# The down product as seven block products in two sets of four banks, its operands streamed

## The chip, the cores and the metric

The kernel runs on one NeuronCore of a Trainium2 chip. The metric is the device time of one execution in microseconds (us), from start to end. Engines are named as in the profile: PE is TensorE (PEld its weight loads), DVE is VectorE, ACT is ScalarE, POOL is GpSimd, SP is SyncE, which issues nearly all transfers.

## What is computed

One layer of an encoder trunk for two request groups g = 0 and 1 (1024 tokens, width 1024), all in float32. The change touches the last third, the feed-forward block:

```python
def conv_glu_ffn(x, w_up, conv_w, conv_b, w_down):
    u = x @ w_up                                  # (1024, 1024) @ (1024, 5632)
    gate, val = jnp.split(u, 2, axis=-1)          # 2816 columns each
    gate = lax.conv_general_dilated(gate, ...) + conv_b     # depthwise, width 3, over tokens
    h = jax.nn.gelu(gate, approximate=False) * val
    return h @ w_down                             # (1024, 2816) @ (2816, 1024)

# in encoder():
x = layer_norm(alpha * x + conv_glu_ffn(x, ...), ln3_g, ln3_b)
```

## The kernel before

Precision: each float32 operand is split into a high part (rounded to the matmul's float32r) and a remainder, and each product is three matmuls: high x high, high x remainder, remainder x high (`mm3`, L128). A split is a copy (ACT or POOL) and a subtraction (DVE or POOL): `split` (L113) and `wsplit` (L120).

The order of the work is the text's, put through a scheduler of the framework, which moves instructions of each engine ahead of others where its own clock says that they are ready first; waits follow from the use of tiles. So the streams of the engines in the trace are not in the order of the text everywhere.

Tiles that matter here: `raw` (L82), three buffers of 4 KB per partition, in which matrices land; `wts` (L1265), six buffers of 8 KB for split weights; fourteen single `slots` of 8 KB (L1270); `resid` (L81), two buffers of 16 KB; PSUM: two each of `pS` (two banks), `pT` and `pO` (one bank), eight banks in all.

The up product (`ffn_up`, L1059) runs over 22 column blocks f of 128 gate and 128 value columns. Each is already computed as seven block products (a scheme with seven instead of eight products of half-size blocks): the blocks of the activation and their sums lie split in the slots; the sums of the weight blocks are made per f in `up_sums` (L1022) from two tiles of `raw` (a11 and a12; a21 and a22), on POOL, and split in `up_weights` (L1041). The products run in the order 6, 1, 7, 5, 2, 4, 3, each 12 matmuls of 128x512; DVE and ACT put the results together (`prod`, L1090). `end` (L1116) makes one block h[f] of 128 features x 1024 tokens in a tile `d` (two buffers) and writes it to DRAM (hD, L1125). During f the weights of f + 1 are made. The working tile of a block (`res`, 16 KB) is one of two that alternate.

The down product (`ffn_down`, L1183) is a plain one. `h_in` (L1163) fetches h[f] (512 KB), splits it with ACT and DVE into a slot; `wd_in` (L1172) fetches two 128-row blocks of one half of w_down's columns, and POOL splits them into `wts`. There are four rounds: (f 0 to 11, columns 0 to 511), (f 0 to 11, columns 512 to 1023), (f 12 to 21, columns 0 to 511), each with f outside and the eight token tiles inside, so that all eight banks are in use; and (f 12 to 21, columns 512 to 1023) with the token tile outside, so that each token tile can be normed and written as it is done (`layernorm`, L798). Each round ends with eight evacuations (`evac`, L1200), DVE operations that add a bank to y; y is loaded from DRAM (yD) at the start, 2 MB twice, and multiplied by the previous norm's gain on DVE.

After the down product of group 0, `phase_in` (L288) of group 1 follows, whose input weights are fetched into `raw` and split into `wts` and whose inputs go to tiles that lie where the slots lay.

## Time and profile before

| what | value |
|---|---|
| median of 3 runs | 3237.38 us (3234.4 to 3240.18) |
| the profiled execution | 3236.86 us, its span 3234.9 us |
| PE busy | 3148.2 us, 97% of the span |
| PEld, DVE, POOL, ACT busy | 83%, 55%, 48%, 38% |
| mean granted clock of PE | 0.989 of full |
| moved by DMA | 351.64 MB, 109 GB/s over the span |
| up product | about 1040 to 1465 us (g = 0), about 2551 to 2988 us (g = 1) |
| down product | about 1465 to 1704 us (g = 0), about 2988 to 3226 us (g = 1) |

The busy line says which engine is in use; the chain of work that ended last says on whose instructions the end depends; the list of waits says for what an engine stood; the timeline shows single instructions with their start and duration. The duration of a matmul there includes its pipeline: its rate is read from the distance of starts.

### The profile page before, as it was taken

What the parts mean: (1) busy time and instruction counts of PE and PEld (TensorE: products, weight loads), DVE (VectorE), ACT (ScalarE), POOL (GpSimd) and SP (SyncE); (2) the same over time, 40 slices, a digit from 0 to 9 for tenths busy, and PEclk for the clock granted to TensorE, in tenths of its full rate; (3) what the DMA queues carried; (4) which work ended last, traced back from release to release, by engine and by line L of the source; (5) the groups of instructions that cost most, each with busy time, mean ns of one, the idle gap of its engine ahead of it and who ended that gap; (6) DMA issues with size and microseconds to landing.
All of it is one profiled execution on the core that took longest, in us unless ns stands there. A gap on an engine that the chain in (4) does not pass through costs nothing.

```text
span 3234.9 us, 43051 instructions
## 1 busy us (share of the span) xinstructions
PE 3148.2 (97%) x16425; PEld 2672.9 (83%) x16425; DVE 1769.0 (55%) x2991; ACT 1217.2 (38%) x2373; POOL 1565.4 (48%) x1165
## 2 busy tenths in 40 slices
PE   8999999999999999999998989999999899999998
PEld 6888889888887888888887889888888788888887
DVE  4152167884536756666235246688444766665614
ACT  2122167882334433331101127687243443333101
POOL 7373512783423655543436451288342465554442
PEclk9999999999999999999999999999999999999999
DMA  8455486003112222236415367501311223224521
GB/s 266 120 150 194 162 219 172 14 8 118 47 52 72 78 81 89 79 111 221 128 55 183 117 169 176 142 17 31 101 49 46 79 78 95 82 79 143 179 95 52
DMA packets 292867, 351.64 MB, mean 109 GB/s; under 512 B 18012, under 2 KB 211764, under 8 KB 291508
## 3 DMA queue, kind: packets, MB, share of 16 engines
q1 hardware_dynamic: 290068, 340.43, 34.7%
q10 hardware_dynamic: 2592, 8.46, 0.7%
q8 instruction: 129, 2.11, 0.3%
q14 instruction: 78, 0.64, 0.1%
HBM read 252.24 MB, written 100.79 MB: 109 GB/s over the span
## 4 chain that ended last, share of the span: by engine, by line
PE 89%; DVE 4%; DMA 3%; POOL 2%; issue 1%; ACT 1%; SPq 0%; ACTq 0%; POOLq 0%; DVEq 0%
PE pS L1095 11%; PE pT L1095 7%; PE pO L1095 7%; PE pO L130 7%; PE pO L132 7%; PE pO L131 7%; PE pT L132 7%; PE pT L130 7%; PE pT L131 7%; PE pO L720 3%; PE pS L693 3%; PE pO L611 3%; PE pT L709 3%; PE pS L132 2%; PE pS L131 2%; PE pS L130 2%
## 5 line engine op out<-in xcount | busy, mean ns | idle before, releaser
L126 POOL TENSOR_TENSOR wts<-raw,wts 128x512 fp32r<-128x512 f32 (+1 forms) x229 | 467.2, 2046 | 239.8 <-ACT wts L109 234.9
L1095 PE MATMUL pS<-t,wts 128*128 128x512 f32 (+1 forms) x1656 | 378.7, 382 | 0.9 <-DVE res L1104 0.9
L1095 PEld LDWEIGHTS pS<-t,wts 128*128 128x128 f32 x1656 | 304.4, 190 | 60.5 <-DVE res L1104 1.6
L130 PE MATMUL pT<-wts,t 128*128 128x512 f32 (+1 forms) x840 | 327.8, 390 | 9.3 <-ACT wts L109 8.9
L130 PE MATMUL pO<-wts,t 128*128 128x512 f32 (+1 forms) x840 | 328.7, 392 | 3.5 <-ACT t L109 2.6
L131 PE MATMUL pO<-wts,t 128*128 128x512 f32 (+1 forms) x840 | 325.5, 388 | 4.2 <-POOL wts L126 4.2
L132 PE MATMUL pO<-wts,t 128*128 128x512 f32 (+1 forms) x840 | 325.6, 388 | 2.9 <-POOL t L126 1.7
L132 PE MATMUL pT<-wts,t 128*128 128x512 f32 (+1 forms) x840 | 325.6, 388 | 0.2 <-POOL t L126 0.2
L131 PE MATMUL pT<-wts,t 128*128 128x512 f32 (+1 forms) x840 | 325.2, 387 | 0.5 <-DVE wts L126 0.5
L1095 PE MATMUL pT<-t,wts 128*128 128x512 f32 (+1 forms) x1104 | 260.3, 385 | 9.8 <-ACT t L109 5.9
L125 POOL TENSOR_SCALAR wts<-raw 128x1024 fp32r<-128x1024 f32 (+1 forms) x88 | 100.6, 1147 | 335.3 <-DMA raw<-w_down 199.7
L1095 PE MATMUL pO<-t,wts 128*128 128x512 f32 (+1 forms) x1104 | 257.2, 382 | 0.4 <-ACT t L109 0.4
L1095 PEld LDWEIGHTS pT<-t,wts 128*128 128x128 f32 x1104 | 204.5, 192 | 50.7 <-ACT t L109 6.3
L1095 PEld LDWEIGHTS pO<-t,wts 128*128 128x128 f32 x1104 | 203.3, 190 | 40.1 <-ACT t L109 0.8
L130 PEld LDWEIGHTS pT<-wts,t 128*128 128x128 f32 x840 | 158.4, 189 | 39.8 <-ACT wts L109 8.9
L132 PEld LDWEIGHTS pO<-wts,t 128*128 128x128 f32 x840 | 158.6, 189 | 35.6 <-POOL t L126 2.2
L130 PEld LDWEIGHTS pO<-wts,t 128*128 128x128 f32 x840 | 158.9, 189 | 35.1 <-ACT t L109 3.9
L131 PEld LDWEIGHTS pO<-wts,t 128*128 128x128 f32 x840 | 158.7, 189 | 35.1 <-POOL wts L126 4.5
L132 PEld LDWEIGHTS pT<-wts,t 128*128 128x128 f32 x840 | 158.3, 188 | 31.8 <-POOL t L126 0.4
L131 PEld LDWEIGHTS pT<-wts,t 128*128 128x128 f32 x840 | 158.4, 189 | 31.4 <-DVE wts L126 1.0
L696 DVE TENSOR_REDUCE mn<-pS 128x1 f32<-128x1024 f32 x128 | 155.9, 1218 | 38.3 <-PE pS L693 36.9
L126 DVE TENSOR_TENSOR wts<-xr,wts 128x512 fp32r<-128x512 f32 x86 | 105.7, 1230 | 107.7 <-ACT wts L109 107.7
(274 smaller groups left out, 6714.7 us busy)
## 6 DMA issues: line engine op xcount, KB each, us to landing
raw<-w_up SPq DMA_DIRECT2D x88, 512.0 KB, 4.1
hD<-d SPq DMA_DIRECT2D x44, 512.0 KB, 5.0
raw<-hD SPq DMA_DIRECT2D x44, 512.0 KB, 3.7
raw<-w_down SPq DMA_DIRECT2D x44, 512.0 KB, 3.7
raw<-w_in SPq DMA_DIRECT2D x32, 512.0 KB, 4.8
kst<-ka SPq DMA_DIRECT2D x32, 512.0 KB, 8.8
qa<-vs SPq DMA_DIRECT2D x16, 512.0 KB, 3.9
ka<-vs SPq DMA_DIRECT2D x16, 512.0 KB, 4.3
```

Of the source, the lines that this page charges most:

```text
L125: nc.gpsimd.tensor_scalar(hi, raw, 1.0, 0.0, op0=ALU.mult, op1=ALU.add)
L126: return (nc.vector if dve else nc.gpsimd).tensor_sub(lo, raw, hi.bitcast(F32))
L130: mm(out, sh, mh, start=start, stop=False)
L131: mm(out, sh, ml, start=False, stop=False)
L132: mm(out, sl, mh, start=False, stop=stop)
L611: nc.tensor.matmul(po[:, n * 64:(n + 1) * 64], pt[:, n, j], v, start=j == 0, stop=j == 1)
L693: nc.tensor.matmul(p[:, ns], q[:, ct * 128:(ct + 1) * 128], ks[:, hl, ns], start=hl == 0, stop=hl == 1)
L696: nc.vector.tensor_reduce(mn, p, axis=X, op=ALU.min)
L709: nc.tensor.transpose(p[:, c * 128:(c + 1) * 128], s[:, k * 128:(k + 1) * 128], self.ident)
L720: nc.tensor.matmul(po[:, :256], bd["v"][:, k, h // 4], hl[l][:, k].rearrange("p a b -> p (a b)"), start=k == 0 and l == 0, stop=k == 7 and ...
L1095: nc.tensor.matmul(p, w[:, x, k], b[l][:, k, cs], start=i in (1, 6, 7, 5) and k + x + l == 0, stop=k == 3 and x == 1, skip_group_check=True)
```

## The change

The down product becomes a product of seven blocks as well. Its operands are halves of the tokens (left, right) by the even and odd 128-row blocks of the 2816 features, and the even and odd row blocks by halves of the columns of w_down. Each of the seven products has 11 steps (one for each pair of row blocks); a step has one 128x512 operand of h (or a sum of such) and one 128x512 operand of w_down (or a sum), and 4 x 3 matmuls.

- `end` collects two blocks d0 and d1; at each odd f it makes three sums of their halves and one difference in place (two on POOL, two on DVE), writes d1 and d0 to hD and the three further blocks to a new DRAM array hS.
- `down_sums`, called at each odd f of group 0 only, fetches two full 128-row blocks of w_down into `raw`, makes four differences in place on POOL, and writes them to a new DRAM array wD, which both groups read.
- `d_in` replaces `h_in` and `wd_in`: for each of the 77 steps it fetches the two operands (two steps at a time into a buffer of `wts`, the first five one at a time into `raw`) and splits both into one slot: one ACT copy of 128x1024, one POOL and one DVE subtraction of 128x512. Up to seven steps are ahead of the matmuls. The slots go round (ten of them for g = 0, fourteen for g = 1).
- The products run in the order 1, 2, 6, 5, 7, 3, 4, alternating between two sets of four banks; products 1, 6, 7, 4 accumulate one upon the other in the first set, 5 and 3 in the second (2 by itself), and after each the four banks are added to y. For g = 1 the last product runs with the token tile outside.
- `layernorm` can take statistics of one half made earlier.

```diff
-            nc.sync.dma_start(hD[f], d)
+            ds.append(d)
+            if f % 2:
+                j, (d0, d1) = f // 2, ds
+                ds.clear()
+                a11, a21, a12, a22 = d0[:, :512], d0[:, 512:], d1[:, :512], d1[:, 512:]
+                s1, s2, s4 = sets[1][:, 3584:], sets[0][:, 3584:], e.u3
+                nc.gpsimd.tensor_add(s1, a21, a22)
+                nc.sync.dma_start(hD[j, 1], d1)
+                nc.gpsimd.tensor_sub(a21, a11, a21)
+                nc.sync.dma_start(hD[j, 0], d0)
+                nc.vector.tensor_sub(s2, s1, a11)
+                nc.vector.tensor_sub(s4, a12, s2)
+                for i, t in enumerate((s1, s2, s4)):
+                    nc.sync.dma_start(hS[j, i], t)
...
+                    if i == 5 and g == 0 and f % 2:
+                        self.down_sums(f // 2, wD)
+                    if f == NFF - 1 and i in (7, 5, 2, 4, 3):
+                        self.d_in(g)
...
+    def down_sums(self, j, wD):
+        nc = self.nc
+        r = []
+        for o in range(2):
+            t = self.raw.tile([128, D], F32, name="raw")
+            nc.sync.dma_start(t, self.a["w_down"][0][(2 * j + o) * 128:(2 * j + o + 1) * 128])
+            r.append(t)
+        b11, b12, b21, b22 = r[0][:, :512], r[0][:, 512:], r[1][:, :512], r[1][:, 512:]
+        nc.gpsimd.tensor_sub(b11, b12, b11)
+        nc.gpsimd.tensor_sub(b12, b22, b12)
+        nc.sync.dma_start(wD[j, 0], r[0])
+        nc.gpsimd.tensor_sub(b22, b22, b11)
+        nc.gpsimd.tensor_sub(b21, b21, b22)
+        nc.sync.dma_start(wD[j, 1], r[1])
+
+    def d_in(self, g):
+        nc = self.nc
+        s = len(self.ds)
+        m, k = divmod(s, self.NK)
+        i = self.SEVEN[m]
+        if not self.dr:
+            n = 1 if s < 5 else min(2, self.NK - k)
+            if s < 5:
+                r = self.raw.tile([128, 1, 2, 512], F32, name="raw")
+            else:
+                r = self.wts.tile([128, 2, 2, 512], F32, name="wts")
+            for x, src in enumerate((self.hsrc[i], self.wsrc[i])):
+                nc.sync.dma_start(r[:, :n, x], src[:, k:k + n])
+            self.dr = [r[:, x] for x in range(n)]
+        r = self.dr.pop(0)
+        ring = (12, 13, 4, 6, 10, 11, 3, 7, 5, 9) + ((8, 0, 1, 2) if g else ())
+        first = (12, 13, 4, 8, 0, 1, 2, 6, 10, 11, 3, 7, 5, 9)
+        t = self.at_slot(first[s] if s < 14 else ring[(s - 14) % len(ring)], [128, 2, 2, 512])
+        self.copy(t[:, 0], r)
+        for x, e in enumerate((nc.gpsimd, nc.vector)):
+            e.tensor_sub(t[:, 1, x], r[:, x], t[:, 0, x].bitcast(F32))
+        self.ds.append(t)
...
+        pa = [self.pA() for _ in range(2)]
+        sets = [[p[:, n * 512:n * 512 + 512] for p in pa for n in range(2)],
+                [self.pT(), self.pO(), self.pT(), self.pO()]]
...
+        def mm(p, m, k, q):
+            i, t = self.SEVEN[m], self.ds[m * self.NK + k]
+            c = slice(q * 128, q * 128 + 128)
+            for x, l in ((0, 0), (0, 1), (1, 0)):
+                nc.tensor.matmul(p, t[:, x, 0, c], t[:, l, 1], start=i in (1, 2, 5) and k + x + l == 0,
+                                 stop=k == self.NK - 1 and x == 1, skip_group_check=True)
...
+        for m, i in enumerate(self.SEVEN):
+            bank = sets[m % 2]
+            if i == 4:
+                gb = self.ln_load(3)
+                if g:
+                    while len(self.ds) < 7 * self.NK:
+                        self.d_in(g)
+                    for q in range(4):
+                        for k in range(self.NK):
+                            mm(bank[q], m, k, q)
+                        finish(q)
+                        evac(i, q, bank[q])
+                        finish(4 + q)
+                    break
+            for k in range(self.NK):
+                s = m * self.NK + k
+                while len(self.ds) < min(s + 7, 7 * self.NK):
+                    self.d_in(g)
+                if m < 2 and 2 <= k < 6:
+                    v = yt(4 * m + k - 2)
                     nc.vector.tensor_mul(v, v, gb[0])
                     nc.vector.tensor_add(v, v, gb[1])
+                if i == 4 and k % 2 and k < 8:
+                    finish(k // 2)
+                for q in range(4):
+                    mm(bank[q], m, k, q)
+            for q in range(4):
+                evac(i, q, bank[q])
+        if not g:
+            for q in range(4):
+                finish(4 + q)
```

`finish` is `layernorm` of one token tile and the write of its output. `SEVEN` is (1, 2, 6, 5, 7, 3, 4), `NK` is 11.

## Rows read from the trace of the kernel before

**Rows 1.** The page: busy time of the engines; the chain that ended last.

```profile
PE 3148.2 (97%) x16425; PEld 2672.9 (83%) x16425; DVE 1769.0 (55%) x2991; ACT 1217.2 (38%) x2373; POOL 1565.4 (48%) x1165
...
PE 89%; DVE 4%; DMA 3%; POOL 2%; issue 1%; ACT 1%; SPq 0%; ACTq 0%; POOLq 0%; DVEq 0%
```

**Rows 2.** Stretches: busy us (instructions) of five engines, clock, DMA share, GB/s.

```profile
1200.00:1300.00 100.00, 100.00 (x443) 82.80 (x442) 61.37 (x64) 39.53 (x60) 56.37 (x37) 1.00 0.25 80
...
1710.00:1720.00 10.00, 8.72 (x30) 6.76 (x30) 9.53 (x7) 3.67 (x4) 10.00 (x6) 0.80 0.80 272
...
3100.00:3200.00 100.00, 100.00 (x443) 82.82 (x442) 30.84 (x46) 7.98 (x7) 44.73 (x26) 1.00 0.21 70
```

**Rows 3.** PE's waits, 1440 to 1725: total us, times, longest; two of four.

```profile
PE pO L131 <- POOL wts L126: 4.2, 1, 4.2
PE pO L132 <- DVE t L115: 1.3, 1, 1.3
...
```

**Rows 4.** Timeline, 1195 to 1240, up product: start, us, instruction, idle before.

```profile
1201.66 9.61 SPq L1028 DMA_DIRECT2D raw<-w_up  x2
...
1200.33 1.30 POOL L126 TENSOR_TENSOR wts<-raw,wts 128x512 fp32r<-128x512 f32 x1 [4.18 <-ACT wts L109]
1205.63 1.29 POOL L1032 TENSOR_TENSOR cs<-raw 128x512 f32<-128x512 f32 x1 [4.00 <-DMA raw<-w_up]
...
1210.83 1.29 POOL L1033 TENSOR_TENSOR xr<-cs,raw 128x512 f32<-128x512 f32 x1
...
1199.77 0.69 DVE L126 TENSOR_TENSOR wts<-cs,wts 128x512 fp32r<-128x512 f32 x1
1201.42 1.29 DVE L1121 SCALAR_TENSOR_TENSOR d<-res,cwt,d 128x1023 f32<-128x1023 f32 x1 [0.97 <-ACT d L1120]
...
1212.82 1.22 DVE L126 TENSOR_TENSOR wts<-xr,wts 128x512 fp32r<-128x512 f32 x1 [2.52 <-ACT wts L109]
...
1212.16 0.63 ACT L109 ACTIVATE wts<-xr 128x512 fp32r<-128x512 f32 x1 [2.00 <-POOL xr L1033]
...
1198.90 5.15 PE L1095 MATMUL pS<-t,wts 128*128 128x512 f32 x22
...
1217.94 5.15 PE L1095 MATMUL pS<-t,wts 128*128 128x512 f32 x22
```

**Rows 5.** Timeline, POOL and DVE, around 1450: two that overlap.

```profile
1448.18 2.41 POOL L126 TENSOR_TENSOR wts<-raw,wts 128x1024 fp32r<-128x1024 f32 x1
...
1448.67 3.00 DVE L1121 SCALAR_TENSOR_TENSOR d<-res,cwt,d 128x1023 f32<-128x1023 f32 x1 [1.36 <-ACT d L1120]
```

**Rows 6.** Timeline: first group's down product begins (PE, SP); PE after its end.

```profile
1456.85 0.39 PE L130 MATMUL pS<-wts,t 128*128 128x512 f32 x1
...
1464.33 2.88 PE L1095 MATMUL pO<-t,wts 128*128 128x512 f32 x12
...
1480.31 0.32 SPq L1125 DMA_DIRECT2D hD<-d  x1
...
1711.11 0.63 PE L132 MATMUL pO<-wts,t 128*128 128x512 f32 x1
1711.54 0.63 PE L130 MATMUL pO<-wts,t 128*128 128x512 f32 x1
```

**Rows 7.** Groups by form, 1480 to 1700: busy us, mean ns, idle before.

```profile
L109 ACT ACTIVATE t<-raw 128x1024 fp32r<-128x1024 f32 x14 | 14.9, 1062 | 109.3 <-PE pO L132 65.6 <-DMA raw<-hD 43.7
```

**Rows 8.** DMA: the page's issues; hD's landing; rates in 1480 to 1620.

```profile
hD<-d SPq DMA_DIRECT2D x44, 512.0 KB, 5.0
...
raw<-w_down SPq DMA_DIRECT2D x44, 512.0 KB, 3.7
...
DMA to landing us min/median/max: 2.6/4.7/10.9
...
GB/s 276 376 401 408 328 13 150 0 234 69 150 167 296 239 50 88 62 139 140 149 181 323 122 150 0 0 0 39 111 149 6 173 222 191 163 54 137 273 150 140
...
res<-yD SPq DMA_DIRECT2D x1, 2048.0 KB, 9.9
```

More of the change, by code (lines that the diff above doesn't have):

```diff
@@ L802, in layernorm @@
         rs = self.small.tile([128, 2], F32, name="brs")
-        st = self.small.tile([128, 2, 6], F32, name="bst")
-        for j in range(2):
+        js = (0,) if st is not None else (0, 1)
+        st = self.small.tile([128, 2, 6], F32, name="bst") if st is None else st
+        for j in js:
             nc.vector.bn_stats(st[:, j], y[:, j * 512:(j + 1) * 512])
@@ L1086, in begin @@
             return e
-        sets, pair = [], []
+        sets, pair, ds = [], [], []
         def prod(e, i, hf=None):
@@ L1183, in ffn_down, with down_src @@
-    def ffn_down(self, B, yD, hD, out):
+    SEVEN = (1, 2, 6, 5, 7, 3, 4)
+    NK = NFF // 2
+    def down_src(self, hD, hS, wD):
+        w = self.a["w_down"][0].rearrange("(j o p) c -> p j o c", p=128, o=2)
+        l, r = slice(0, 512), slice(512, D)
+        hv, sv, tv = [t.rearrange("j i p c -> p j i c") for t in (hD, hS, wD)]
+        self.hsrc = {1: hv[:, :, 0, l], 2: hv[:, :, 1, l], 6: sv[:, :, 1], 5: sv[:, :, 0],
+                     7: hv[:, :, 0, r], 3: sv[:, :, 2], 4: hv[:, :, 1, r]}
+        self.wsrc = {1: w[:, :, 0, l], 2: w[:, :, 1, l], 6: tv[:, :, 1, r], 5: tv[:, :, 0, l],
+                     7: tv[:, :, 0, r], 3: w[:, :, 1, r], 4: tv[:, :, 1, l]}
@@ L1184, in ffn_down @@
+    def ffn_down(self, g, yD, out):
         nc, a = self.nc, self.a
@@ L1205, in evac @@
                 nc.vector.tensor_add(v, v, p)
-        for lo, hi, n in ((0, K0, 0), (0, K0, 1), (K0, NFF, 0)):
-            bank = []
-            for _ in range(2):
-                p = self.pA()
-                bank += [p[:, :512], p[:, 512:], self.pT(), self.pO()]
-            if (lo, n) != (0, 0):
-                self.wd = [None] * (lo // 2)
-            for f in range(lo, hi):
-                if lo == n == 0 and 2 <= f < 2 + NT:
-                    v = yt(f - 2)
+            if i == 7:
+                stats[ct] = self.small.tile([128, 2, 6], F32, name="bs7")
+                nc.vector.bn_stats(stats[ct][:, 1], v)
@@ new lines, in finish @@
+        def finish(ct):
+            self.layernorm(yt(ct), gb, 896 if g and ct >= NT - 2 else 0, stats.get(ct))
+            nc.scalar.dma_start(out[ct * 128:(ct + 1) * 128], yt(ct))
+        for m, i in enumerate(self.SEVEN):
[18 more added lines that the diff above has]
+                    v = yt(4 * m + k - 2)
@@ L1218, in ffn_down @@
                     nc.vector.tensor_mul(v, v, gb[0])
                     nc.vector.tensor_add(v, v, gb[1])
-                if f % 2 == 0 and f // 2 >= len(self.wd):
-                    self.wd_in(n)
-                if n == 0:
-                    while len(hs) <= f:
-                        self.h_in(hD)
-                elif len(hs) < NFF - 1 and len(hs) - 12 <= f - (3 if f > 4 else 0) and not 4 < f < 8:
-                    self.h_in(hD)
-                for ct in range(NT):
-                    mm(bank[ct], f, ct, self.wd, f == lo, f == hi - 1)
@@ L1230, in ffn_down @@
-            for ct in range(NT):
-                evac(bank[ct], ct, n, lo == 0)
-        gb = self.ln_load(3)
-        self.wd = [None] * (K0 // 2)
-        for f in range(K0, NFF, 2):
-            self.wd_in(1, 2 if f == NFF - 2 else None)
-        for ct in range(NT):
-            p = self.pB()
-            for f in range(K0, NFF):
-                mm(p, f, ct, self.wd, f == K0, f == NFF - 1)
-            evac(p, ct, 1, False)
-            self.layernorm(yt(ct), gb, 896 if ct >= NT - 2 else 0)
-            nc.scalar.dma_start(out[ct * 128:(ct + 1) * 128], yt(ct))
+                if i == 4 and k % 2 and k < 8:
+                    finish(k // 2)
@@ L1286, in run @@
                 if "mid" in stages:
[L1287 removed]
+                    yD = dt(f"yD{g}", [NT, 128, D])
+                    hD, hS = dt(f"hD{g}", [NFF // 2, 2, 128, T]), dt(f"hS{g}", [NFF // 2, 3, 128, 512])
                     B, todo = self.phase_mid(g, S, o2s, ob, G, U, yD)
                 if "ffn" in stages:
[L1290 to L1291 removed]
+                    self.ffn_up(g, B, todo, hD, hS, wD)
+                    self.ffn_down(g, yD, a["out0" if g == 0 else "out1"])
             if stages[-1] != "ffn":
```

43 lines of the change are left out of this document (11 added, 32 removed).

## The prediction

> **What bounds the kernel now.** First read is the page's busy line and the shares of the chain that ended last: TensorE is busy 97% of the span and carries 89% of the chain [rows 1]. So the next views are those that say whether TensorE ever waits in the stages that the change touches. In the up product and in the down product it is busy without a break: 100 us of every 100, 443 matmuls each, at full clock [rows 2]. The list of TensorE's waits from the end of the first up product to beyond the first down product has four entries, 6.3 us together, and all lie behind the last down matmul, where the second request group begins [rows 3]; there the clock also falls [rows 2]. So both stages are pure counts of matmuls: what takes matmuls away is worth its full time until some other engine or a queue ends last. The next view is the timeline of one step of the up product. Consecutive steps start at 1198.90 and 1217.94, thus 19.04 us for 84 matmuls (7 products of 12) or **0.2267 us per matmul** [rows 4].
>
> **What is removed.** The down product of one request group now takes 22 x 8 x 2 x 3 = 1056 matmuls, 239.4 us. After, 7 products x 11 steps x 4 x 3 = 924, 209.5 us. The shape is the same (128x128 stationary, 512 columns moving), so I take the same pace. That is 132 x 0.2267 = 29.9 us per group, **-59.9 us** for both.
>
> **The stream in the down product.** After, a step of 12 matmuls lasts 2.72 us and needs 512 KB fetched and one split: an ACT copy of 128x1024 at 1.06 us [rows 7], a GpSimd subtraction of 128x512 at 1.30 us and a VectorE one at 0.69 us (both when alone [rows 4]). Each fits in 2.72 us, with 7 steps of lead. The fetch is 512 KB in 2.72 us, 193 GB/s; in the present down product the queues moved up to 408 GB/s in slices [rows 8]. No cost in steady state. The evacuations fall from 32 to 28 per group and each bank set now has a whole product (30 us) for its four; they cost nothing, and nothing before either, as TensorE never waited on them [rows 3].
>
> **The start of the down product.** Five steps are ready and the next four come through free weight buffers. Step 9, however, needs the left operand of the last pair of columns. Its present counterpart was written out from 1480.31 [rows 6]. After, a GpSimd addition and a subtraction (1.30 each) come ahead: issue 1482.9, landed 5.0 later, the fetch 3.7 [rows 8], ACT 1.06 and GpSimd 1.30: ready at about 1494. The last up product started at 1464.33 [rows 6] and some 2.5 us of down matmuls had already been slipped in by then; so step 9 is due at about 1464.5 + 9 x 2.72 = 1489. 5 us late, unless matmuls of the second product, which need nothing of that pair, stand in front. The kernel's scheduler did reorder across stages like that: a down matmul (its first at 1456.85) stands ahead of the last up product [rows 6]. Bounds 0 to +8 per group (the 5, and a half-clock stretch behind it, priced as below); I take 1.5, **+3 us**. The loads of y (2 MB, 9.9 us each [rows 8]) must now also wait for the sums' writes. They are queued on SP ahead of fetches, and VectorE's multiplications of y by the gain stand ahead of later splits. A rival below.
>
> **The up product: sums of h.** Per pair of column blocks GpSimd gets 2 operations and VectorE 2 more, SP three more writes, 768 KB. Nobody in this stage waits for them but the two d buffers: the block after next can't begin its d before d0 is written, and ACT's copies are queued behind that. Two GpSimd operations and a 5.0 us write end about when the next use comes (19 us after the last); bank reuse leaves a step of slack. Cost with the next item.
>
> **The up product of the first group: sums of the weights.** Four more GpSimd operations per pair, two loads, two writes, and two more tiles from `raw`, which has three. This is the part I trust least. In the trace the ring of three is already what times the weights: the second w_up load of a step goes out (1201.66) the moment GpSimd's split at 1200.33 has released the tile three allocations back; the sum on it starts at 1205.63, the second at 1210.83, ACT's copy at 1212.16, VectorE's remainder ends at 1214.04, and TensorE wants the product at 1217.94 [rows 4]. 3.9 us of slack. After, in every odd step the tile released at 1201.66 goes to a w_down row block instead. On the same clock: load 3.7 -> 1205.4, GpSimd 1.30 -> 1206.7, write, 5.0 as hD's -> 1211.7, only then the w_up load, 4.0 as from 1201.66 to 1205.63 -> 1215.7 (the first two from [rows 8]), two sums 2.6 -> 1218.3, ACT 0.63, VectorE 0.69 to 1.22: 1219.6 to 1220.2. So the first product of the step is **about 2 us late instead of 3.9 early**. Product 1, which needs the other tile, can run first and takes 2.72 us; then nothing is lost. Ten pairs have a step behind them: bounds 0 and +40 (2.2 late and nearly as much again in turns with VectorE); I take 0.8 us a pair, **+8 us**, nearer to the covered end, as the scheduler reorders.
>
> **The turns of VectorE and GpSimd.** While GpSimd's subtraction ran from 1448.18 to 1450.59, VectorE's operation started at 1448.67 and took 3.00 us instead of its 1.29 [rows 4]: it ended 1.1 us behind GpSimd [rows 5]. They take turns. One step of the up product has 7 GpSimd operations at 1.29 (9.0 us) and 4 x 0.69 + 3 x 1.29 (6.6 us) on VectorE with both inputs from tiles in SBUF [rows 4]: 15.6 of 19.04 us, 31.2 of 38.1 per pair. After, the first group adds 6 x 1.30 + 2 x 0.69 = 9.2: **40.4 of 38.1**; the second adds 4.0: 35.2. Up to 1.1 us of each VectorE operation's end evidently lies outside the turn, so the true sum is smaller. Bounds 0 and +25 (2.3 x 11); I take **+2 us**. The Trainium skill, "SBUF — State Buffer", section "Who interferes with whom", has a rule that speaks against the change: a VectorE instruction with two SBUF inputs and a GpSimd instruction that reads SBUF lock each other out fully. The 3.00 us row agrees. By that rule with whole durations the sum would have +25 here, without it 0.
>
> **The end of the first group.** Now the first weights of the next group are split only at the last matmul, since the w_down tiles sit in their buffers until then: 6.3 us of waits [rows 3], and 10 matmuls at about 0.427 instead of 0.2267 (1711.11 to 1711.54), some 2 us [rows 6], at a mean granted clock of 0.80 of 2.4 GHz, thus partly at 1.2 [rows 2]. After, these buffers hold raw data and are done with some 16 us before the end. Against that, four whole layer norms come after the last matmul, GpSimd about 2.4 each, by its 128x1024 operation [rows 5]. Bounds -8 and +6; I take **-4 us**. The end of the second group keeps its chain: evacuation, one statistics half, norm, write.
>
> **Sum.** -59.9 + 3 + 8 + 2 - 4 = -51. The profiled execution took 3236.86 us (span 3234.9 and 2.0 around it), the median of the runs shown is 3237.38, 0.5 above: no correction beyond that. 3237.4 - 51 = **3186 us**.
>
> **Rivals.** *The ring and the turns hidden*: -59.9 + 3 - 4, **3176**. For it: TensorE has no wait at all now [rows 3]. *The ring not covered*: products stay in their order, 4 us for each of ten pairs: -59.9 + 3 + 40 + 2 - 4, **3218**. For it: 3.9 us of slack is all there is [rows 4]. *The turns bind*: +25 in place of 2, **3209**; against it, bank evacuations and ACT's work run beside. *The start starves*: both y loads (19.8 us) ahead of the fetches use up the 7 steps of lead (19 us) and some 10 us per group are lost: -51 + 20, **3206**; against it, before, the stage starts with the same loads and no wait. *Slower than before*: the chain of w_down load, sum, write, w_up load through `raw` sets the step. All other terms give -58.9, so it decides from 5.9 us a pair. With a write at the slowest landing of hD seen, 10.9 instead of 5.0 [rows 8], product 1 not moved: (2.2 + 5.9) x 10 = 81, **3260**. For it, 768 KB and 2 MB more per pair share the queue; against it, DMA moves only about 80 GB/s in this stage [rows 2].
>
> **How the numbers follow.** Forecast 0.40, hidden 0.20, ring uncovered 0.13, turns 0.13, starved start 0.05, slower 0.08; 0.01 for anything else. The range takes the hidden case with the full gain at the group's end and the uncovered ring with a few us more: 3168 to 3228. A measurement of this kernel tells about 0.2% (6.5 us) from no change. Faster 0.87, same 0.04 (the ring between 5 and 6.5 us a pair), slower 0.09.
>
> **What would show it.** Right: 924 matmuls per down product at 0.2267 without a wait; first up product 419 us plus under 20; waits of TensorE on weight splits in odd steps only, and only in the first group. Wrong: waits within the down product on a split or a fetch (the stream does not keep up), waits in the second group's up product (then it is the sums of h or the turns, not the ring), or VectorE and GpSimd both busy without a gap.

## The result, and the profile after

The changed kernel takes 3296.86 us (median of 4 runs, 3293.94 to 3297.42) where the kernel before took 3238.51 beside it: a ratio of 1.018 with the interval 1.0163 to 1.0198. It is **slower by 58 us** where 51 us less was forecast; 3296.86 lies far above the range. The profiled execution took 3297.42 us, its span is 3295.6.

The page of after, engines and chain, to set against [rows 1]:

```profile
PE 3124.1 (95%) x16161; PEld 2640.9 (80%) x16161; DVE 1929.7 (59%) x3135; ACT 1325.8 (40%) x2483; POOL 1831.7 (56%) x1317
...
PE 72%; DMA 8%; POOL 7%; DVE 6%; issue 4%; ACT 2%; SPq 1%; POOLq 0%; ACTq 0%; DVEq 0%
```

The 264 matmuls are gone (16425 to 16161), but PE's busy time fell by 24 us, not by 60: many of those left took longer. Its share of the chain fell from 89% to 72%, and DMA, POOL and DVE took it over. So PE now waits. Where, the list of its waits over the whole span says (total us, times, longest):

```profile
PE pS L1096 <- DVE res L1105: 42.8, 20, 5.0
PE pS L1257 <- ACT t L109: 23.4, 2, 12.8
PE pS L1257 <- POOL t L1233: 17.6, 2, 9.1
...
PE pO L130 <- ACT t L109: 3.1, 1, 3.1
...
PE pO L132 <- DVE t L115: 1.7, 1, 1.7
```

Before, neither stage had such waits ([rows 3] for the time from 1440 on; the few us at the very start of an up product stand in both kernels). L1096 is the up product, L1257 the down product. The last two rows stand at the end of the first group, as in [rows 3]: 4.8 us there, where four before made 6.3. In stretches (columns as in [rows 2]; the first three are the first up product and the start of the first down product, then its steady state, then the second group's up product):

```profile
1200.00:1300.00 100.00, 89.83 (x378) 72.42 (x377) 67.09 (x62) 32.81 (x50) 70.00 (x45) 0.97 0.40 135
1560.00:1580.00 20.00, 4.08 (x7) 1.95 (x7) 20.00 (x21) 10.02 (x10) 13.52 (x1) 0.50 0.99 372
1580.00:1600.00 20.00, 18.72 (x72) 15.31 (x73) 12.54 (x12) 6.37 (x6) 20.00 (x14) 0.84 0.77 278
1640.00:1660.00 20.00, 20.00 (x90) 16.57 (x89) 8.40 (x12) 8.01 (x8) 12.34 (x8) 1.00 0.57 186
2700.00:2800.00 100.00, 100.00 (x443) 82.79 (x442) 70.75 (x71) 38.82 (x60) 65.63 (x43) 1.00 0.32 108
```

Two separate losses are seen. The first group's up product, the only one with sums of weights, does 378 matmuls in 100 us instead of 443; the second group's has no loss. And the down product is at full pace in its steady state (90 matmuls in 20 us), but its start nearly stands still, with the clock at 0.50 (1.2 GHz).

The starts of the matmuls say how much each loss is. From its first matmul to its last, the first group's up product lasts 499.0 us instead of 438.6 (1030.3 to 1529.3, before 1028.2 to 1466.8); the second's lasts 437.1 instead of 436.8. From the last up matmul to the last down matmul, 237.6 us pass instead of 237.3 in the first group, and 236.4 instead of 237.4 in the second. So the starts of the down products eat nearly the whole 60 us of matmuls that were taken away, and the first up product adds 60. Besides, 15.1 us pass from the last matmul to the end of the span, where 9.5 did.

**The up product.** A timeline of 1237 to 1280 in after (start, us, instruction, idle before it), one place of many:

```profile
1237.63 0.34 SPq L1200 DMA_DIRECT2D raw<-w_down  x1
...
1251.95 0.33 SPq L1200 DMA_DIRECT2D raw<-w_down  x1
1255.19 1.38 POOL L1204 TENSOR_TENSOR raw<-raw 128x512 f32<-128x512 f32 x1 [1.05 <-DMA raw<-w_down]
1256.60 0.33 SPq L1205 DMA_DIRECT2D wD<-raw  x1
1259.27 0.38 SPq L1029 DMA_DIRECT2D raw<-w_up  x1
1263.96 1.29 POOL L1033 TENSOR_TENSOR cs<-raw 128x512 f32<-128x512 f32 x1 [4.31 <-DMA raw<-w_up]
1266.52 1.15 ACT L109 ACTIVATE wts<-cs 128x512 fp32r<-128x512 f32 x2 [7.96 <-POOL cs L1035]
1271.14 0.57 ACT L109 ACTIVATE res<-pS 128x512 f32<-128x512 f32 x1
1271.61 2.31 DVE L1122 SCALAR_TENSOR_TENSOR d<-res,cwt,d 128x1023 f32<-128x1023 f32 x1
1273.96 1.28 DVE L1123 SCALAR_TENSOR_TENSOR d<-res,cwt,d 128x1023 f32<-128x1023 f32 x1
1275.16 0.68 DVE L1105 TENSOR_TENSOR res<-res,pS 128x512 f32<-128x512 f32 x1
1275.89 4.28 PE L1096 MATMUL pS<-t,wts 128*128 128x512 f32 x11 [2.90 <-DVE res L1105]
```

Read it downwards. The first w_down tile is loaded at 1237.63. The second finds a free buffer only at 1251.95; the first tile's second sum (L1204) has to wait for it, only then is that tile written (1256.60), and only then can the w_up load that is to use its buffer go (1259.27). A buffer of three is held for 21.6 us. GpSimd idles 4.31 us for that load, ACT 7.96. It is the chain of the prediction, twice as long. What PE then waits for, however, is not a weight: ACT's and DVE's late splits and the operations of `end` stand ahead of the copy of product 1's bank (1271.14) and of the addition of product 6's (L1105) in their queues, and PE waits 2.90 us for the bank.

**The start of the down product**, first group, timeline of 1535 to 1600:

```profile
1534.72 18.97 PE L1257 MATMUL pS<-t 128*128 128x512 f32 x83
1566.46 1.22 PE L1257 MATMUL pS<-t 128*128 128x512 f32 x2 [12.76 <-ACT t L109]
...
1581.28 7.39 PE L1257 MATMUL pS<-t 128*128 128x512 f32 x21 [8.48 <-POOL t L1233]
...
1543.45 0.32 SPq L1137 DMA_DIRECT2D hD<-d  x1
1545.18 0.57 SPq L1243 DMA_DIRECT2D res<-yD  x1
1547.67 0.61 SPq L1243 DMA_DIRECT2D res<-yD  x1
1548.34 4.45 SPq L1224 DMA_DIRECT2D wts<-hD  x2
...
1557.64 4.63 DVE L1298 TENSOR_TENSOR res<-res,lng 128x1024 f32<-128x1024 f32 x4 [13.67 <-DMA lng<-ln_g]
1562.18 4.63 DVE L1299 TENSOR_TENSOR res<-res,lnb 128x1024 f32<-128x1024 f32 x4
1566.72 4.63 DVE L1298 TENSOR_TENSOR res<-res,lng 128x1024 f32<-128x1024 f32 x4
1571.26 0.69 DVE L1233 TENSOR_TENSOR t<-wts,t 128x512 fp32r<-128x512 f32 x1
...
1565.35 2.00 ACT L109 ACTIVATE t<-wts 128x1024 fp32r<-128x1024 f32 x2 [26.43 <-DMA wts<-hD]
```

The fetch that step 9 needs is issued at 1548.34, behind the last pair's writes and both loads of y, and ACT can copy it at 1565.35: 17.0 us. By then DVE is at twelve multiplications and additions of y by the gain, 1.16 us each and 13.9 together, ahead of its first split (1571.26). What that does to GpSimd's first split, two more views show: its own row in the timeline, and the durations of such operations at the second group's start (shortest, median and longest in ns):

```profile
1566.48 14.74 POOL L1233 TENSOR_TENSOR t<-wts,t 128x512 fp32r<-128x512 f32 x1 [23.06 <-ACT t L109]
...
L1233 POOL TENSOR_TENSOR t<-wts,t x30: 1266/1737/15382, 3078.7 to 3139.6; 128x512 fp32r<-128x512 f32 x30
```

One subtraction of 128x512 took 14.74 us, where the like took 1.30 in [rows 4]. DVE worked without a gap until 1580.11, on the gain and on splits of its own; GpSimd's operation ended at 1581.22, and PE's wait of 8.48 us with it, at 1581.28. So GpSimd got no turn until DVE's run of operations was over. The second group's start has the same waits (10.6 and 9.1 are their longest), and one subtraction of 15.38 us.

### The profile page after: what moved, and what is told of

Read it like the earlier page. It is cut to its first block, busy times and chain, and to the rows that moved or that the text cites. A ratio compares the mean times of both kernels' runs of the same rounds, so it can differ in the third digit from the quotient of the medians.

```text
span 3295.6 us, 43553 instructions
## 1 busy us (share of the span) xinstructions
PE 3124.1 (95%) x16161; PEld 2640.9 (80%) x16161; DVE 1929.7 (59%) x3135; ACT 1325.8 (40%) x2483; POOL 1831.7 (56%) x1317
## 4 chain that ended last, share of the span: by engine, by line
PE 72%; DMA 8%; POOL 7%; DVE 6%; issue 4%; ACT 2%; SPq 1%; POOLq 0%; ACTq 0%; DVEq 0%
PE pS L1096 6%; PE pO L132 5%; PE pO L130 5%; PE pO L131 5%; PE pT L132 5%; PE pT L130 5%; PE pT L131 5%; PE pS L1257 5%; PE pT L1096 4%; PE pO L1096 4%; PE pO L720 3%; PE pO L1257 3%; PE pT L1257 3%; PE pS L693 3%; PE pO L611 3%
## 5 line engine op out<-in xcount | busy, mean ns | idle before, releaser
L1096 PE MATMUL pS<-t,wts 128*128 128x512 f32 (+1 forms) x1656 | 399.4, 394 | 42.8 <-DVE res L1105 42.8
L126 POOL TENSOR_TENSOR wts<-raw,wts 128x512 fp32r<-128x512 f32 (+1 forms) x187 | 361.7, 1940 | 130.7 <-ACT wts L109 128.6
L1096 PEld LDWEIGHTS pS<-t,wts 128*128 128x128 f32 x1656 | 313.5, 197 | 113.0 <-DVE res L1105 51.0
L1233 POOL TENSOR_TENSOR t<-wts,t 128x512 fp32r<-128x512 f32 x144 | 264.6, 1850 | 141.6 <-ACT t L109 129.0
L1257 PE MATMUL pS<-t 128*128 128x512 f32 x1056 | 249.0, 396 | 43.2 <-ACT t L109 23.4
L1257 PEld LDWEIGHTS pS<-t 128*128 128x128 f32 x1056 | 201.6, 191 | 88.8 <-ACT t L109 24.2
L1096 PE MATMUL pT<-t,wts 128*128 128x512 f32 (+1 forms) x1104 | 262.1, 387 | 7.9 <-ACT t L109 5.9
L1096 PE MATMUL pO<-t,wts 128*128 128x512 f32 (+1 forms) x1104 | 259.1, 384 | 0.4 <-ACT t L109 0.4
L130 PE MATMUL pT<-wts,t 128*128 128x512 f32 (+1 forms) x640 | 250.1, 391 | 8.3 <-ACT wts L109 8.3
L130 PE MATMUL pO<-wts,t 128*128 128x512 f32 (+1 forms) x640 | 251.1, 392 | 3.7 <-ACT t L109 3.1
L109 ACT ACTIVATE t<-wts 128x1024 fp32r<-128x1024 f32 x144 | 150.8, 1058 | 252.2 <-PE pO L1257 85.0
L132 PE MATMUL pO<-wts,t 128*128 128x512 f32 (+1 forms) x640 | 248.4, 388 | 3.3 <-DVE t L115 1.7
L131 PE MATMUL pT<-wts,t 128*128 128x512 f32 (+1 forms) x640 | 247.5, 387 | 0.5 <-DVE wts L126 0.5
L131 PE MATMUL pO<-wts,t 128*128 128x512 f32 (+1 forms) x640 | 247.9, 388 | 0.0
L132 PE MATMUL pT<-wts,t 128*128 128x512 f32 (+1 forms) x640 | 247.6, 387 | 0.0
L1096 PEld LDWEIGHTS pT<-t,wts 128*128 128x128 f32 x1104 | 206.3, 194 | 49.8 <-ACT t L109 6.3
L1096 PEld LDWEIGHTS pO<-t,wts 128*128 128x128 f32 x1104 | 204.5, 192 | 40.4 <-ACT t L109 0.8
L1233 DVE TENSOR_TENSOR t<-wts,t 128x512 fp32r<-128x512 f32 x144 | 139.9, 990 | 137.8 <-ACT t L109 135.8
L125 POOL TENSOR_SCALAR ptb<-praw 128x512 fp32r<-128x512 f32 x116 | 75.6, 652 | 160.7 <-ACT praw L109 160.0
L720 PE MATMUL pO<-ptb,v 128*128 128x256 f32 x1024 | 164.5, 296 | 0.1
## 6 DMA issues: line engine op xcount, KB each, us to landing
kst<-ka SPq DMA_DIRECT2D x32, 512.0 KB, 10.3
```

Source lines behind the costliest of these rows:

```text
L109: self.nc.scalar.activation(out, in_, AF.Copy)
L126: return (nc.vector if dve else nc.gpsimd).tensor_sub(lo, raw, hi.bitcast(F32))
L130: mm(out, sh, mh, start=start, stop=False)
L131: mm(out, sh, ml, start=False, stop=False)
L132: mm(out, sl, mh, start=False, stop=stop)
L720: nc.tensor.matmul(po[:, :256], bd["v"][:, k, h // 4], hl[l][:, k].rearrange("p a b -> p (a b)"), start=k == 0 and l == 0, stop=k == 7 and ...
```

## The experiments

Three theories for the up product: **chain** (a raw tile is held from load through sum to write, the next w_up load waits), **turns** (four more GpSimd operations in turns with DVE), **sums of h** (they crowd the queues). Three for the down start: **late pair** (writes of the last pair of h and its sums), **loads of y ahead of the fetches**, and **gain operations ahead of the splits**. The number given of each run is its difference to the kernel before on the same chip (after: +58.4); runs of the kernel before lie between 3230.52 and 3245.25, so a difference of less than some 8 us in a single run tells little. There the length of the first group's up product, read as above, tells more (438.6 us before, 499.0 after).

### One part of the sums of weights at a time

`e1`: no sums of weights; products 6, 5, 7 and 4 stream plain slices of w_down (another output).

```diff
-                    if i == 5 and g == 0 and f % 2:
-                        self.down_sums(f // 2, wD)
```

> Leaves the weight sums out altogether (no loads, differences or writes in the first group's up product; products 6, 5, 7 and 4 stream plain slices of w_down of the same size instead, so what is computed differs). The changed kernel waits 42 us in the first group's up product, nearly all on the evacuation on line 1105, and its first up product is some 60 us longer than before. Theory A (ring: w_down tiles through raw delay the w_up loads, and late weight splits stand ahead of evacuations on ACT and DVE) and theory B (turns: four more GpSimd operations a pair fill the shared time of DVE and GpSimd) both expect the up product back at the length it had before, within 5 us, and 3237 to 3245 us in all. Theory C (sums of h do it) expects 3285 or more. The down product's start keeps its stalls of some 24 us per group in all three.

Measured: 3236.62, **-0.1**. Behind the first steps the up product has no wait above 0.4 us, and it lasts 437.6 us, as before; the down products start as badly as in after (11.0 and 9.1). So the sums of weights cost 58 us, all in the up product, and, these gone, the starts still eat nearly the whole 60 us of matmuls.

`e2`: the loads and writes through `raw` stay, the four subtractions go (the first tile's write then no longer waits for the second tile; another output).

```diff
-        nc.gpsimd.tensor_sub(b11, b12, b11)
-        nc.gpsimd.tensor_sub(b12, b22, b12)
...
-        nc.gpsimd.tensor_sub(b22, b22, b11)
-        nc.gpsimd.tensor_sub(b21, b21, b22)
```

> Keeps the loads of w_down into raw and the writes to wD, leaves out the four GpSimd differences (so wD holds plain rows and what is computed differs). A (ring): most of the loss stays, 3275 to 3297 us, waits on line 1105 of 25 to 42 us. B (turns): the loss goes, 3237 to 3250 us, waits under 8 us.

Measured: 3241.06, **+4.4**. PE waits 4.5 us in eight pieces on L1105, and the up product lasts 442.8 us. Occupying the ring with a load and a write is nearly free, against theory A.

`e3`: the four GpSimd operations on data of their own, 128x512 each, without `raw` and DMAs (another output).

```diff
-                        self.down_sums(f // 2, wD)
+                        for _ in range(4):
+                            nc.gpsimd.tensor_sub(t, ib, ib)
```

> The counterpart: no w_down tile in raw, no loads and no writes, but four GpSimd differences of 128x512 on data of their own at the same place of the text (products 6, 5, 7 and 4 stream plain slices of w_down, so what is computed differs). A (ring): 3237 to 3255 us, waits under 10 us. B (turns): 3275 to 3297 us, waits of 25 to 42 us.

Measured: 3245.41, **+8.7**. Its up product (columns as in [rows 2]):

```profile
1200.00:1300.00 100.00, 100.00 (x443) 82.82 (x442) 75.40 (x71) 38.15 (x58) 80.01 (x53) 1.00 0.33 108
```

PE is busy without a break while DVE and GpSimd are busy 75.40 and 80.01 of 100 us, more than in after (67.09 and 70.00). The up product lasts 438.5 us, against 437.6 in e1: turns alone fall, these engines had the time; in after they idle and are then late.

`e12`: after, with the four operations on one column each (medians of 0.2 to 0.7 us instead of 1.3 to 1.7), so that the waits of the chain stay and its work goes (another output).

```diff
-        nc.gpsimd.tensor_sub(b11, b12, b11)
+        nc.gpsimd.tensor_sub(b11[:, :1], b12[:, :1], b11[:, :1])
```

> The changed kernel with the four GpSimd differences of a pair on one column instead of 512 (so wD is nearly plain w_down and what is computed differs): the loads, the writes and the order in which each waits for the other stay, GpSimd's work goes. Theory A' (the wait of the first raw tile for the second's load and the write): waits on line 1105 of 20 us or more, 3265 us or more. Theory D' (GpSimd's four operations inside that chain, and their turns with DVE, are needed for it): waits under 12 us, 3237 to 3252 us.

Measured: 3277.31, **+36.9**. The list of PE's waits, and GpSimd's timeline in it:

```profile
PE pS L1096 <- DVE res L1105: 28.8, 16, 3.6
...
1249.29 0.19 POOL L1204 TENSOR_TENSOR raw<-raw 128x1 f32<-128x1 f32 x1 [1.40 <-DMA raw<-w_down]
...
1257.29 1.29 POOL L1033 TENSOR_TENSOR cs<-raw 128x512 f32<-128x512 f32 x1 [6.88 <-DMA raw<-w_up]
```

With almost no work in the four operations, 36.9 of the 58.4 us between e1 and after remain (the up product lasts 481.2 us), and GpSimd stands 6.88 us for a w_up load. Beyond e2 there are only the waits: the first tile is held for the second, and GpSimd's queue stands for loads of w_down.

`e8`: each raw tile holds 256 columns of all four blocks; all the work stays, no tile waits for another.

```diff
+        for q in range(2):
+            t = self.raw.tile([128, 2, 2, 256], F32, name="raw")
+            for o in range(2):
+                nc.sync.dma_start(t[:, o], src[:, o, :, qs])
+            b11, b12, b21, b22 = t[:, 0, 0], t[:, 0, 1], t[:, 1, 0], t[:, 1, 1]
```

> Complete kernel. As the changed one, but each of the two raw tiles of a weight sum holds 256 columns of all four blocks, so that no tile waits for the other's load before it can be written and released; the same differences on GpSimd (eight of 256 columns), the same bytes, through the same three raw buffers. Neither the ring alone (+4 us against the kernel without weight sums) nor the operations alone (+9 us) made the loss of 60 us. Theory A' (chain: the first tile is held until the second has landed, been summed and written; only then can the weights of the next step be fetched): waits on line 1105 fall from 42 to under 12 us, 3240 to 3255 us. Theory D (no single chain: GpSimd's operations and the sums of h together delay every release): waits stay over 25 us, 3275 to 3297 us.

Measured: 3261.43, **+22.7**. Its PE waits:

```profile
PE pS L1096 <- DVE res L1105: 21.0, 20, 2.4
```

The wait between the tiles is taken away, and little else (GpSimd's work comes as eight smaller operations, the transfers as eight instead of four). PE's waits halve (42.8 to 21.0), and the loss falls from 58.4 to 22.7, between the two ranges expected; the up product lasts 463.4 us. A buffer is held for 16.1 us instead of 21.6 (from a load at 1224.6). So 36 of the 58 us go with the tile that is held for the other.

`e4`: the sums of weights stay, the sums of h go (products 6, 5 and 3 read plain halves; another output).

```diff
-                nc.gpsimd.tensor_add(s1, a21, a22)
...
-                    nc.sync.dma_start(hS[j, i], t)
+            nc.sync.dma_start(hD[f // 2, f % 2], d)
```

> Keeps the weight sums as in the changed kernel, leaves the sums of h out (each block of h written as it is made, no hS; products 6, 5 and 3 stream plain halves of h, so what is computed differs). A and B: the first up product stays at least 40 us longer than before. C: it comes back, 3240 us or less. All: without the writes of the sums the loads of y may go out 4 us earlier, so the start of each down product loses 0 to 6 us less.

Measured: 3228.96, **-7.7**: 66 us less than after.

```profile
PE pS L1242 <- DVE res L1250: 14.7, 3, 8.1
PE pS L1096 <- DVE res L1105: 8.7, 11, 1.3
PE pS L1096 <- DVE wts L126: 6.5, 4, 3.3
```

These two waits of the up product are 15 us, and the down starts no longer wait for a fetch. The up product lasts 462.1 us, 23.5 more than before, so it met neither expectation (40 or more, or none); the two down stretches last 220.1 and 221.1 us, some 16 less than in after each, where 0 to 6 were expected. So the sums of h are not free either: alone they cost the up product nothing (e1), together with the chain they do. Nor is a held buffer enough by itself: here one is held even longer than in after (25.2 us, from the load at 1222.48 to that at 1247.67). The full loss in the up product takes both, and no part adds up with the others; that each uses slack which the next would have needed is our reading.

### The start of the down product

`e5`: y and gain loaded and multiplied one product later. `e6`: the sixteen gain operations left out (another output).

```diff
+                if (m, k) in ((0, 6), (1, 2)):
+                    nc.sync.dma_start(y[m], yD[4 * m:4 * m + 4].rearrange("c p d -> p c d"))
+                if m in (1, 2) and 2 <= k < 6:
...
-                    nc.vector.tensor_mul(v, v, gb[0])
-                    nc.vector.tensor_add(v, v, gb[1])
```

> The changed kernel with the loads of y and of the gain put behind the fetches: the first half of y at step 6 of the first product, the second at step 2 of the second, the multiplications by the gain at steps 2 to 5 of the second and third products, the first product's evacuation behind them. Theory S (the start starves because 4 MB of y and 1 MB of gain go out ahead of the fetches of steps 9 and on, and 16 multiplications stand ahead of splits on DVE): the waits at the start of a down product fall from some 24 us to under 5 us per group, and with the half clock behind them the time falls by 45 to 55 us, to 3242 to 3252 us. Theory H (the last pair of column blocks of h is written too late by itself): a wait of 10 us or more stays in each group, 3265 us or more.

> The changed kernel without the 16 DVE multiplications and additions of y by the gain (so what is computed differs); loads as they are. S, with its two halves apart: the wait on the fetch stays (10 to 13 us per group), the wait on the GpSimd remainder behind it (8.5 and 9.1 us) goes; 3270 to 3282 us. If only the transfers matter: 3290 us or more.

Measured: e5 3282.73, **+41.9**; e6 3271.61, **+30.8**. In e6 the wait of 8.5 and 9.1 us on GpSimd's split is gone, the 13.1 on the fetch stays. In e5 the fetch's wait falls to 5.4, but DVE's split is late instead (10.0 in two): the gain has only moved, and the 45 to 55 us expected did not come. In e6 the long subtraction is gone with the gain (GpSimd's splits at the first start):

```profile
L1233 POOL TENSOR_TENSOR t<-wts,t x32: 1288/1743/1797, 1518.7 to 1619.8; 128x512 fp32r<-128x512 f32 x32
```

The longest takes 1.80 us. After, e1, e2, e3, e8, e12 and e13 have one of 14.7 to 15.5 us at each start; in the other runs no GpSimd operation takes more than 4 us. So what the gain costs at its place is in part that GpSimd stands still beside it.

`e13`: one line, s2 into a tile that is free earlier, to write the last pair sooner.

```diff
-                s1, s2, s4 = sets[1][:, 3584:], sets[0][:, 3584:], e.u3
+                s1, s2, s4 = sets[1][:, 3584:], e.u2, e.u3
```

> The changed kernel with one line altered: s2 of h lies in e.u2 instead of the spare end of the other block's buffer, so that buffer, which y's first half takes, is free some 20 us earlier. Theory S (y's loads ahead of the fetches starve the start): 2 MB less stand ahead of the fetches; the wait on ACT's copy falls from 12.8 and 10.6 us to 3 to 7 us, and the first four multiplications are done earlier, so the wait on the GpSimd remainder falls by half or more; 3262 to 3280 us. If the fetch waits for the last blocks of h alone: the first wait stays over 9 us, 3285 us or more.

Measured: 3292.97, **+52.5**; the waits at the start stay (10.3 and 9.1 in the first group, 6.6 and 9.1 in the second). That buffer held the fetch by a few us at most.

`e9`: the last two steps of products 1 and 2 put behind the first nine of both, y late. `e10`: that, with the sums of weights moved as in e7 below. `e11`: e10 with the line of e13, y's first half early and its second in product 3.

```diff
+    STEPS = ([(0, k) for k in range(9)] + [(1, k) for k in range(9)] + [(m, k) for m in range(2) for k in (9, 10)]
+             + [(m, k) for m in range(2, 7) for k in range(11)])
```

> The changed kernel with y and gain late as before and, besides, the last two steps of products 1 and 2 (the only ones that need the last pair of column blocks of h) put behind the first nine of both. The weight sums stay in the up product with their 42 us. Theory H+S (the pair is written too late, and y's transfers and multiplications finish the job): under 5 us of waits at the start of each down product, 3240 to 3252 us. If the start is starved for another reason (buffers of wts not free, GpSimd and DVE in turns too slow for 2.7 us a step): waits of 10 us or more stay, 3265 us or more.

> Complete kernel: steps reordered and y late, and the weight sums beside the cross-attention's preparation, on DVE, with tiles of their own. With all three causes away the 59.9 us of matmuls should be left: 3180 to 3195 us. Were something else lost in the sums of h or in the stream: 3200 to 3226 us.

> Complete kernel: as the one with steps reordered and the weight sums beside the cross-attention's preparation, but the sum s2 of h lies in the work area of its own block (e.u2), so the first half of y no longer waits for the last sum's write and is loaded and multiplied at the start (steps 2 to 5), and the second half is loaded and multiplied only within the third product. In the kernel before this one DVE multiplied the second half ahead of the first product's evacuation, and TensorE waited 15 to 21 us for that evacuation. Expected if that and the fetch queue are all that is left: waits under 8 us per down product, 3180 to 3200 us. If the DVE and GpSimd turns bind at the start whatever the order: 3205 us or more.

Measured: e9 3301.98, **+63.3**; e10 3234.74, 0.9985 (0.9976 to 0.9993); e11 3227.52, 0.9963 (0.9949 to 0.9976). The fetch is no longer waited for, but PE then waits for product 1's banks: in e11 20.1 us at once in the second group, since all of DVE's work on y came ahead of the evacuation. The scheduler issued y's second load as soon as its tile was free (1494.93), however late it stands in the program. More reordering gained nothing over e7, and none of the three came near the lower range expected of it.

### A version that loses nothing in the up product, and what then is left

`e7`: the sums of weights beside the cross preparation, on DVE and in four tiles of their own; y late as in e5.

```diff
+            self.dsm = P("dsm", 4)
...
-            t = self.raw.tile([128, D], F32, name="raw")
+            t = self.dsm.tile([128, D], F32, name="dsm")
...
-        nc.gpsimd.tensor_sub(b11, b12, b11)
+        nc.vector.tensor_sub(b11, b12, b11)
```

> Complete kernel: loads of y late as above, and the weight sums made before, beside the cross-attention's preparation (4 tiles of their own instead of raw, the four differences on DVE, which is busy a quarter of that stage). If A or B and S hold: the first up product as long as before, no starved starts, 3237 - 60 + 5 to 15: 3182 to 3197 us. If the sums of h cost by themselves, or the preparation stage has no room: 3205 to 3230 us.

Measured: 3225.94, ratio **0.9953** (0.9937 to 0.997): half a percent faster than before, in the slower of the two ranges expected. Its up product, and the waits of its down products:

```profile
1200.00:1300.00 100.00, 100.00 (x442) 82.81 (x442) 67.57 (x66) 37.60 (x59) 66.80 (x45) 1.00 0.29 94
...
PE pT L1260 <- DVE t L1239: 18.1, 4, 6.1
...
PE pS L1260 <- ACT t L109: 7.2, 2, 4.3
```

Its up product lasts 436.4 us. Against e5, only the sums of weights differ (their place, engine and tiles): 56.8 us, the up product's loss once more.

`e14`, `e15`, `e16`: e7 without the gain operations (as e6), without the sums of h (as e4), and without either; all three give another output.

> The version with the sums of w_down beside the cross preparation and y later, and the sixteen VectorE multiplications and additions of y by the gain left out (the output is not the layer norm's any more). That version took 3225.9, some 45 us more than the count of matmuls gives. If VectorE's work on y, in turns with GpSimd's remainders, is what holds the down products' starts: 3205 to 3213, and TensorE's waits on VectorE's split of the operands (8.6 us) vanish. If the late writes of h and of its sums hold them, and the gain only fills that time: 3219 to 3226, the same waits under another name.

> The version with the sums of w_down beside the cross preparation and y later, without the sums of h: products 6, 5 and 3 read plain halves of h (another output), seven products as before, no hS written. If the late writes of the last pair hold the start of the down products: 3205 to 3212, and the wait on the left operand's copy (4.3 us) vanishes. If VectorE's work on y holds it: 3219 to 3226 with the 8.6 us wait kept.

> The version with the sums of w_down beside the cross preparation and y later, with neither the sums of h nor the gain's sixteen operations (both left out, another output). If these two together are the whole of what the down products' starts lose: 3185 to 3198, with at most 2 us of waits of TensorE in a down product. If the loads of y and of the next phase in SP's queue ahead of the fetches keep a share, or half clock does: 3200 to 3212 with waits on copies of fetched operands.

Measured beside 3240.66: e14 3200.95, **-39.7** (0.9873, 0.9858 to 0.9888); e15 3211.2, **-29.5** (0.9909, 0.9894 to 0.9924); e16 3188.19, **-52.5** (0.9837, 0.9818 to 0.9857). In the first group's start e14 keeps one wait of 3.6 us on the fetched operand, e15 one of 8.7 us on an evacuation behind DVE's work on y, e16 none. The start of e16, which streams the same seven products:

```profile
1490.00:1510.00 20.00, 20.00 (x90) 16.58 (x89) 15.05 (x14) 6.07 (x6) 13.34 (x8) 1.00 1.02 381
1510.00:1530.00 20.00, 20.00 (x90) 16.58 (x89) 7.89 (x9) 9.43 (x9) 14.26 (x9) 1.00 1.04 390
```

90 matmuls in every 20 us with the queues full (381 and 390 GB/s): the stream as such loses nothing. From e7, the gain costs 25 us, the sums of h 15, both 38: here the parts do add up. From the last up matmul to the last down matmul, 229.4 and 230.2 us pass in e7, 214.1 and 215.3 in e14, 219.1 and 222.9 in e15, and 208.5 and 209.6 in e16, which is what the prediction counted for 924 matmuls (209.5).

## Why the prediction was wrong

**Right: the matmuls.** 924 per down product at 0.2267 us in the steady state, nothing lost to the stream or to the evacuations of the two bank sets; e16, without the gain and the sums, has its down products last 208.5 and 209.6 us and is 52.5 us faster than before.

**Failed: "Product 1, which needs the other tile, can run first and takes 2.72 us; then nothing is lost", and with it 0.8 us a pair.** Measured: 58 us over the first group's pairs (after against e1), near the 5.9 us a pair from which the slower rival decided. Two things were wrong in that step. First, the hold: 10 us were counted from the w_down load to the w_up load into the same buffer (1201.66 to 1211.7), 21.6 were seen. The prediction let the first tile be written after one sum of its own; in the code its second sum needs the second tile, and that waits for a buffer of the same ring. Without it 36 of the 58 us go (e8 against after), and with hardly any work left in the chain 37 remain (e12); but it costs so much only together with the sums of h (e4). Second, the victim: what comes late at PE is not a weight but the evacuation of a bank, behind the late splits on ACT and DVE. In the place shown, running another product first does not help, since it is the queue that is late and not the operand alone.

**Failed: the price of the sums of h by itself.** That "bank reuse leaves a step of slack" holds where they are alone (second group: no loss). In the first group the chain uses that slack too; without the sums the waits fall from 43 to 15 us (e4). The prediction put the cost of these sums into the next item, where no term for them stands.

**Failed: the start of the down product, +3 for both groups.** Step 9 was put 5 us late; PE waited 12.8 us for it and soon after 8.5 more. Two terms of that sum were mis-sized. One is the fetch: 3.7 us there, 17.0 here, as it stands behind 4 MB of y and the writes on SP. The other is GpSimd's subtraction behind it: 1.30 there, 14.74 here, beside DVE's run of gain operations. The turns of the two engines, priced for the up product alone, struck here. The rival for the starved start named those loads and priced them at 20 us with a chance of 5%; measured, y's place costs about 16 (after to e5), the gain's operations 25 and the sums of h 15 (e7 to e14 and e15). What was held against it, that before the stage starts with the same loads and no wait, did not carry over; that this is because the new product needs a fetch and its splits in every step is our reading, and no run tests it.

**The smaller terms.** The turns in the up product, +2, were right: with the four operations alone it lasts 438.5 us, against 437.6 without them (e3, e1), far from the 25 that full turns would have cost. The first group's end, -4, stays open: the waits are 4.8 us instead of 6.3, but from the last down matmul to the next group's first up matmul 840.1 us pass in after, 847.1 before, and 847.0 in e16, whose end is the same as in after. The second group's end, which "keeps its chain" at no cost in the prediction, takes 5.6 us more (15.1 instead of 9.5).

**The account.** Of the two profiled spans (3234.9 and 3295.6, +60.7), the first up product makes +60.4, the two down stretches -0.7 in place of -59.9, and the end +5.6; the rest, -7.0 between the groups and +2.4 elsewhere, is not explained. e16 shows the same from the other side: its span is 46.5 us shorter, the two down stretches make -56.6 and the first up product -3.0, but that product begins 8.4 us later, with the sums in the preparation (1036.6 instead of 1028.2), and the end takes 5.1 us more. Either loss alone would have taken nearly all of the gain; the slower rival had the mechanism of the first, but not the second.

## What to carry to other kernels

When a stage takes on more work, ask which instruction stands behind the new one in each engine's queue, and not only whether the new data is in time: here the operand was ready and the bank's evacuation was not. A buffer of a ring that is held from a load through a computation to a write costs its whole chain, and more where one tile waits for the next (21.6 us here, where 10 were counted); give such work a pool of its own and a stage in which its engine idles. And the gain of a shorter stage is first spent at its start: list everything queued ahead of its first fetch, and look for a long run of VectorE work with two inputs in SBUF beside the GpSimd operation that the start waits for.

## What the runs showed of the hardware

- **Busy time does not tell who is the bound.** DVE and GpSimd at 75.40 and 80.01 of 100 us left PE without a wait (e3); at 67.09 and 70.00 PE stood still for a tenth of the time (after).
- **The turns are not even.** Beside DVE's run of gain operations, which kept 1.16 us each, one GpSimd subtraction of 128x512 took 14.74 us instead of 1.30 [rows 4]; without the gain the longest took 1.80 (e6). In e11, at the second group's start, the two kinds did take turns: four of DVE's took 8.91 us together, and GpSimd's up to 2.25 each. The Trainium skill, "SBUF — State Buffer", section "Who interferes with whom", calls the pair of ports that the two engines share an exclusive lock; the rows agree, and here GpSimd was shut out not for one DVE instruction but for more than ten in a row.
- **A wait costs more than its length.** Around the waits of 12.8 and 8.5 us the granted clock was 0.50 in 1560 to 1580 and 0.84 in the next 20 us; in the up product, with waits of up to 5 us, 378 matmuls kept PE busy for 89.83 us, 0.2376 each, at a clock of 0.97, against 0.2257 at full clock in [rows 2].
